# Layer A's attention: one sum product for two heads, and one store of a unit's two outputs into one tensor

## The chip, the core and the metric

The kernel runs on one core of a Trainium2 chip. The metric is the device time of one execution in microseconds (us), the median of several runs; lower is better.

## What is computed

A decoder trunk of two layers on one sequence of 2048 positions, model width 1024, all in float32. Layer A, where the change lies, is attention with a forget gate over 16 heads of width 64. Cut to what matters:

```python
# layer A
u = rmsnorm(h, norm_a_g)
q, k, v, f_logit, gate = jnp.split(u @ w_in_a, [1024, 2048, 3072, 3088], axis=-1)
q, k = rmsnorm(q.reshape(b, s, 16, 64), qnorm_g), rmsnorm(k.reshape(b, s, 16, 64), knorm_g)
c = jnp.cumsum(log_sigmoid(f_logit + b_forget), axis=1)
logits = q k^T / 8 + c[query] - c[key];  causal mask
o = softmax(logits) v
h = h + (o * silu(gate)) @ w_out_a
```

Layer B then computes a shared key/value projection, sliding-window attention and its own projection in the same style. Nothing of layer B's computation is changed.

## The kernel before

TensorE multiplies in fp32r. To keep float32 accuracy, an operand is split into a rounded high part and a rest, and a product is made of three: high by high, high by rest, rest by high. Tensors that do not fit on chip are spilled to DRAM and loaded again.

Layer A goes through four stages. **Projections** (`projections`, products at L759 and L722): q, k and v of all heads go to the DRAM tensors `qa`, `ka`, `va`, the running sums of the forget gate to `ca`, and the normed input to `ut`. **Attention** (`attention_a`): per head, four units of 512 queries (`CH`), per unit 2, 4, 6 or 8 steps of two key blocks of 128. A step makes the scores (L978, L979, with a mask added by a product with the identity matrix, L983 and L987), their exponentials on ScalarE (L984, L993), the high part (L996, ScalarE) and the rest (L997, GpSimd) of those, their running sum on VectorE (L1006), and three steps later the values products (L1021). Row maxima for heads further on are made beside it (L933, L941, L946) and are written into a row of the query operand by small transfers (`big<-m`, L560, four per unit). The **gate** (`gate()`, L1063) is a filler: its products are dealt out between the steps, and its weights come in through 62 loads of 512 KB into two `wr` buffers (`wr<-wg`, L1040).

At the end of a unit the sum of the exponentials is folded. VectorE's transposing reduction (L897) leaves in `part` 32-query pieces on 128 partitions; per head, `recips` makes one product with the constant `fold` (L906, 64 rows of 32), multiplies by `roots` (L911), takes the reciprocal (L912) and stores it to the DRAM tensor `rd` (L913). The last head does this in two parts. In the same place the unit's values leave PSUM by a ScalarE copy (L1029) into a tile of 128 rows: the upper 64 rows are the main part, the lower 64 the correction from the low part of v. They go out as two stores, to the DRAM tensors `om` (L1031) and `oc` (L1032), each [1024, 2048], 64 rows per head.

In the **output projection** (`out_a`, products at L1244) a step handles a chunk of 512 positions and a pair of heads, 32 steps in all. `gated_load` loads for a pair four tiles of 128 x 512: `m` from `om` (L1179), `c` from `oc` (L1180), the gate (L1181) and the reciprocals, spread over 64 rows each (L1184, two loads). `gated` adds m and c on GpSimd (L1198), multiplies by the reciprocals (L1199) and the gate (L1202), and splits the result (L1203, L1204) into the operand. Loads run five steps ahead and prepared operands two (`Pairs`); the first three pairs are loaded, and two of them prepared, within attention (L1198 to L1204 on GpSimd there). The residual x is loaded (L1229) and the result stored to `h1` (L1257) in the same stage.

All transfers are issued by SP in one queue, in order. The order on every engine is set when the program is built, by a scheduler that places instructions by its own estimates: when a product or a transfer goes away, its neighbours may change places.

Of the kernel before, what the change touches and what calls it, by code (L numbers as in the profile page):

```python
# [14 lines left out]
BF16 = mybir.dt.bfloat16  # L15
# [8 lines left out]
P = 128  # L24
S = 2048
# [126 lines left out]
class Trunk:  # L152
# [7 lines left out]
    def __init__(self, ctx, tc, a, out):  # L160
        self.ctx, self.tc, self.nc, self.a, self.out = ctx, tc, tc.nc, a, out
        dr = ctx.enter_context(tc.tile_pool(name="dram", bufs=1, space=DRAM))
        self.d = {
            name: dr.tile(shape, F32, name=name, tag=name)
            for name, shape in (
                ("qa", [H, P, S]),
                ("ka", [H, P, S]),
                ("va", [H, S, P]),
                ("ca", [2, H, S]),
                ("ut", [NCH, 2, NDT, P, CH]),  # L170
                ("wg", [NDT, P, 4, 2, 2, P]),
                ("gt", [D, S]),
                ("om", [D, S]),
                ("oc", [D, S]),
                ("rd", [H, S]),
                ("rr", [2, S]),
                ("h1", [S, D]),
                ("qb", [H, P, S]),
                ("kb", [NKV, P, S]),
                ("vb", [NKV, S, P]),  # L180
                ("gtb", [D, S]),
            )
        }
# [25 lines left out]
    def constants(self):  # L209
        nc, cp, a = self.nc, self.const, self.a  # L210

        def select(view, src, pattern, base, cm, fill):
            nc.gpsimd.affine_select(
                out=view, in_=src, pattern=pattern, compare_op=ALU.is_ge,
                fill=fill, base=base, channel_multiplier=cm,
            )

        def tile_(name, shape, dt=F32):
            return cp.tile(shape, dt, name=name, tag=name)

# [12 lines left out]
        self.identb = tile_("identb", [P, P], BF16)  # L233
        nc.vector.tensor_copy(self.identb, self.ident)

        self.mask_s = tile_("mask_s", [P, 2, P], BF16)
        nc.gpsimd.memset(self.mask_s, 0.0)
        for i in range(2):
            select(self.mask_s[:, i], self.mask_s[:, i], [[1, P]], 0, -1, NEG)

        self.band = tile_("band", [P, 2, P], BF16)
        nc.gpsimd.memset(self.band[:, 0], 0.0)
        select(self.band[:, 0, :], self.band[:, 0, :], [[-1, P]], 0, 1, NEG)
        nc.vector.tensor_tensor(self.band[:, 1], self.tri, self.ident, ALU.subtract)

        self.loads = []
        warm = tile_("warm", [P, 1])
        nc.scalar.activation(warm, self.ones[:, :1], AF.Sqrt)

        def vector(name, n, views):  # L250
            t = tile_(name, [P, n])
            for rows, src in views:
                self.loads.append((t[rows], src))
            return t

        def column(name, src, n):
            return vector(name, n, [(slice(0, P), src.rearrange("(t p) -> p t", p=P))])

        def pair_column(name, src):
            col = src.rearrange("(p o) -> p o", o=1)  # L260
            return vector(name, 1, [(slice(0, HD), col), (slice(HD, P), col)])

        def row(name, src, n):
# [585 lines left out]
    def attention_a(self, op):  # L849
# [12 lines left out]
            fill=NEG, base=0, channel_multiplier=1,  # L862
        )
        NSB = CH // 32
        part = self.sb("part", [P, 2, NCH, NSB], bufs=1)

        roots = self.sb("ro1", [NCH * NSB, 2, 32])
        heads, state = {}, {}
        units = [(h, ch) for h in range(H) for ch in range(NCH)]
        steps = [(u, p) for u, (h, ch) in enumerate(units) for p in range(2 * ch + 2)]  # L870
# [23 lines left out]
        def sums(u):  # L894

            h, ch = units[u]
            nc.vector.tensor_reduce(  # L897
                part[:, h % 2, ch, :], state[u][0].rearrange("p (b i) -> p b i", i=32),
                AX.X, ALU.add, apply_transpose=True,
            )  # L900

        def recips(h, c0=0, c1=NCH):

            nr = (c1 - c0) * NSB
            ps = self.ps("sc", [nr, 32])
            nc.tensor.matmul(  # L906
                ps, part[:, h % 2, c0:c1].rearrange("p c b -> p (c b)"), self.fold,
                start=True, stop=True,
            )
            rc = self.sb("sq", [nr, 32])  # L910
            nc.vector.tensor_tensor(rc, ps, roots[:nr, 1 if c0 else 0], ALU.mult)  # L911
            nc.vector.reciprocal(rc, rc)  # L912
            nc.sync.dma_start(  # L913
                out=d["rd"][h, c0 * CH : c1 * CH].rearrange("(b i) -> b i", i=32), in_=rc
            )

        def max_pieces(h, ch):
# [44 lines left out]
        def scores(n, u, p):  # L962
# [17 lines left out]

            if last:
                o = tiles[0].rearrange("p (b q) -> p b q", b=2)[:, :, :P]
                nc.tensor.matmul(o, self.identb, self.mask_s, start=False, stop=True)  # L983
                nc.scalar.activation(pf[:, :tw], tiles[0][:, :tw], AF.Exp, scale=HD**-0.5)  # L984
            else:
                for n_, ps in enumerate(tiles if diag else ()):
                    mm = nc.tensor.matmul(  # L987
                        ps[:, :P], self.identb, self.mask_s[:, 0], start=False, stop=True
                    )
# [21 lines left out]
        def values(item):  # L1011
# [14 lines left out]
            if last:  # L1026
                state.pop(u)
                ov = self.sb("sq", [P, CH])
                nc.scalar.copy(ov, pv)  # L1029
                rows, cols = slice(h * HD, (h + 1) * HD), slice(ch * CH, (ch + 1) * CH)  # L1030
                nc.sync.dma_start(out=d["om"][rows, cols], in_=ov[:HD, :])  # L1031
                nc.sync.dma_start(out=d["oc"][rows, cols], in_=ov[HD:, :])  # L1032

        def closes(item):
            u, p = item[:2]
# [58 lines left out]
        for c in range(2):  # L1094
            rows = roots[: (NCH - c) * NSB, c]
            nc.sync.dma_start(out=rows, in_=d["rr"][0, c * CH :].rearrange("(b i) -> b i", i=32))
            nc.vector.reciprocal(rows, rows)
        more_pieces(1)
        per = len(pieces)

# [32 lines left out]
        for n, (u, p) in enumerate(steps):  # L1133
# [12 lines left out]
            if p == 2 * ch + 1:  # L1146
                if h == H - 1 and ch in (0, NCH - 1):
                    due.append((n + SUM_LAG, (h, ch and 1, ch + 1)))
                elif ch == NCH - 1:
                    due.append((n + SUM_LAG, (h,)))  # L1150
            while due and due[0][0] <= n:
                recips(*due.pop(0)[1])
            feed((total - KEPT) * (n + 1) // len(steps), pause=True)
# [21 lines left out]
    def gated_load(self, ch, p, tiles):  # L1175
        nc, d = self.nc, self.d
        rows, cols = slice(p * P, (p + 1) * P), slice(ch * CH, (ch + 1) * CH)
        m, c, g, rb = tiles
        nc.sync.dma_start(out=m, in_=d["om"][rows, cols])  # L1179
        nc.sync.dma_start(out=c, in_=d["oc"][rows, cols])  # L1180
# [25 lines left out]
    def out_a(self, op, res, dst, ahead, fetch, norm):  # L1206
# [12 lines left out]
        for s in range(NCH * NDT):  # L1219
# [9 lines left out]
                nc.sync.dma_start(out=xr[:, p - 1], in_=res[t0 : t0 + P, :])  # L1229
            if s == NDT:  # L1230

                self.gk16 = self.sb("part", [P, ROT], bufs=1)
# [394 lines left out]
```

## Time and profile before

| | |
|---|---|
| Median of 3 runs | 2440.47 us (2437.79 to 2440.94) |
| Profiled execution | 2441.27 us, of which the span of the profile is 2439.5 us |
| Granted TensorE clock | 1.00 throughout |
| Attention (scores from 594 to 1434 us) | 595 to 1448 us |
| Output projection, first and last product | 1450.4 to 1626.3 us |
| SP: a store to `om`, a store to `oc`, a 128-row store to `gt` | medians 472, 588 and 326 ns of SP's time |

The span is the time from the first instruction to the last on the core. Busy time is the union of an engine's instructions; TensorE's ends are modelled, so its busy time says that it was fed, not that it ran at its peak. A row of a chain gives the start, the length and the engine, tile and line of a piece; the chain is followed back from the last instruction, at each step to what released it. A row of the waits reads: who waited, for whom, us in total, how often, the longest.

### The profile page before, as it was taken

The numbers are of one execution on the slowest core, as the hardware profiler recorded it, in microseconds if no ns is written. First come the engines' busy times: TensorE is split into PE (matmuls) and PEld (weight loads), VectorE is DVE, ScalarE is ACT, GpSimd is POOL, SyncE is SP. The second block draws the span as 40 slices with busy tenths as digits, with TensorE's granted clock in tenths as the row PEclk, the third lists the DMA queues.
The fourth block names the chain that finished last, engine by engine and source line by source line (L and its number), as shares of the span: only waits on it lengthen the run. The fifth ranks groups of instructions, "written<-read, shape, count | busy, mean of one in ns | idle before, by whom it ended". The sixth has DMA issues, their size and how long they took to land.

```text
span 2439.5 us, 36263 instructions
## 1 busy us (share of the span) xinstructions
PE 2407.4 (99%) x11952; PEld 2024.2 (83%) x11952; DVE 1729.3 (71%) x4098; ACT 1260.6 (52%) x2504; POOL 998.2 (41%) x643
## 2 busy tenths in 40 slices
PE   8999999999999999999999999999999999999999
PEld 6788899988888788888888778888888888788887
DVE  7656667735889888888988865556666523777776
ACT  5433324323878778777877761135322312555554
POOL 0000000011878777777878852200011000377775
PEclk9999999999999999999999999999999999999999
DMA  6656555677554655575466549965433425555552
GB/s 182 207 168 184 157 154 168 197 233 235 171 168 127 207 156 147 147 212 172 130 195 174 169 145 311 300 225 159 126 103 106 139 69 161 178 180 179 178 181 74
DMA packets 351517, 419.24 MB, mean 172 GB/s; under 512 B 64929, under 2 KB 248257, under 8 KB 345153
## 3 DMA queue, kind: packets, MB, share of 16 engines
q1 hardware_dynamic: 351328, 416.92, 57.2%
q8 instruction: 95, 1.56, 0.3%
q14 instruction: 94, 0.76, 0.1%
HBM read 265.29 MB, written 151.40 MB: 171 GB/s over the span
## 4 chain that ended last, share of the span: by engine, by line
PE 86%; DMA 5%; DVE 4%; ACT 2%; issue 1%; POOL 1%; SPq 1%; ACTq 0%; DVEq 0%; POOLq 0%
PE b L759 27%; PE pa L1021 10%; PE pb L1063 7%; PE b L1244 5%; PE pb L1457 5%; PE sc L978 5%; PE sc L979 5%; PE mx L933 5%; PE pb L722 3%; PE b L722 3%; PE pa L1387 2%; PE b L1308 2%; DMA wr<-wg 1%; PE pa L1244 1%; PE pb L1244 1%
## 5 line engine op out<-in xcount | busy, mean ns | idle before, releaser
L759 PE MATMUL b<-wh,big 128*128 128x512 f32 (+3 forms) x2560 | 774.1, 375 | 9.4 <-ACT wh L486 8.8
L997 POOL TENSOR_TENSOR big<-st,big 128x1024 fp32r<-128x1024 f32 (+1 forms) x320 | 655.4, 2067 | 242.5 <-ACT big L996 160.3
L759 PEld LDWEIGHTS b<-wh,big 128*128 128x128 f32 x2560 | 472.3, 189 | 82.2 <-ACT wh L486 10.9
L759 PE MATMUL b<-wl,big 128*128 128x512 f32 (+3 forms) x1280 | 474.9, 371 | 1.9 <-DVE wl L487 1.9
L1006 DVE TENSOR_TENSOR ac<-ac,st 128x512 f32<-128x512 f32 (+3 forms) x576 | 352.7, 612 | 51.7 <-ACT st L993 24.7
L993 ACT ACTIVATE st<-sc 128x512 f32<-128x512 f32 (+1 forms) x512 | 273.7, 583 | 117.8 <-PE sc L979 49.5
L1021 PE MATMUL pa<-big 128*128 128x512 f32 (+3 forms) x1280 | 319.9, 365 | 0.9 <-POOL big L997 0.9
L996 ACT CAST big<-st 128x1024 fp32r<-128x1024 f32 (+1 forms) x320 | 295.2, 923 | 8.5
L759 PEld LDWEIGHTS b<-wl,big 128*128 128x128 f32 x1280 | 241.9, 189 | 38.2 <-DVE wl L487 5.9
L1021 PEld LDWEIGHTS pa<-big 128*128 128x128 f32 x1280 | 229.2, 190 | 39.6 <-POOL big L997 2.7
L946 DVE TENSOR_REDUCE mt<-mx 128x1 f32<-128x384 f32 (+1 forms) x360 | 214.2, 598 | 29.5 <-PE mx L933 26.8
L495 ACT ACTIVATE sq<-b,r 128x512 f32<-128x512 f32 (+2 forms) x128 | 77.8, 608 | 301.1 <-PE b L759 298.2
L978 PE MATMUL sc<-big 128*128 128x512 f32 (+3 forms) x640 | 232.9, 368 | 0.1
L979 PE MATMUL sc<-big 67*128 67x512 f32 (+3 forms) x640 | 229.3, 367 | 0.0
L933 PE MATMUL mx<-big 66*128 66x512 f32 (+2 forms) x600 | 224.3, 379 | 0.2
L1063 PE MATMUL pb<-wh,wr 128*128 128x512 f32 x488 | 178.4, 398 | 4.2 <-DMA wr<-wg 4.0
L497 DVE TENSOR_REDUCE sm<-sq 128x8 f32<-128x512 f32 (+2 forms) x128 | 74.9, 585 | 138.4 <-ACT sq L495 138.2
L859 POOL MEMSET rot<- 128x512 bf16 x1 | 0.5, 524 | 421.2 <-PE pb L349 421.2
L1356 POOL TENSOR_TENSOR big<-big,tri 128x1024 fp32r<-128x1024 f32 x60 | 143.8, 2396 | 69.4 <-DVE big L1353 64.5
L941 DVE CUSTOM_DVE_ANT_0 mx<-mx,rot 128x384 f32<-128x384 f32 (+2 forms) x240 | 147.0, 617 | 20.7 <-PE mx L933 19.3
L978 PEld LDWEIGHTS sc<-big 128*128 128x128 f32 x640 | 121.7, 190 | 22.0 <-DVE st L542 0.5
L510 POOL TENSOR_TENSOR ro<-qn,rot 128x64 f32<-128x64 f32 (+1 forms) x48 | 15.6, 326 | 299.4 <-DVE qn L501 299.4
(281 smaller groups left out, 4226.5 us busy)
## 6 DMA issues: line engine op xcount, KB each, us to landing
wr<-wg SPq DMA_DIRECT2D x62, 512.0 KB
va<-st SPq DMA_DIRECT2D x32, 512.0 KB
ka<-st SPq DMA_DIRECT2D x64, 256.0 KB
ut<-big SPq DMA_DIRECT2D x16, 1024.0 KB
big<-ka SPq DMA_DIRECT2D x16, 1024.0 KB
big<-qa SPq DMA_DIRECT2D x16, 1024.0 KB
qb<-st SPq DMA_DIRECT2D x64, 256.0 KB
big<-qb SPq DMA_DIRECT2D x16, 1024.0 KB
```

The costliest lines, as they stand in the source:

```text
L759: nc.tensor.matmul(ps[:, :n], u[tb // 4][:, dt, us], W[k][dt], start=(dt == 0 and i == 0), stop=(dt == NDT - 1 and i == 2),)
L933: mm = nc.tensor.matmul(ps, qb[:66, i * P : (i + 1) * P], kb[:66, k0:k1], start=True, stop=True,)
L946: nc.vector.reduce_max(o, ps, axis=AX.X)
L978: nc.tensor.matmul(o, ka[:, ks], qa[:, qs], start=not (last and n_), stop=False)
L979: nc.tensor.matmul(o, kb[:, ks], qb[:, qs], start=False, stop=not diag)
L993: nc.scalar.activation(pf[:, off : off + w], ps[:, :w], AF.Exp, scale=HD**-0.5)
L996: nc.scalar.copy(ph[:, :tw], pf[:, :tw])
L997: nc.gpsimd.tensor_tensor(pl[:, :tw], pf[:, :tw], f_(ph[:, :tw]), ALU.subtract)
L1006: nc.vector.tensor_tensor(a_, a_, pf[:, off : off + w], ALU.add)
L1021: nc.tensor.matmul(pv[:, q0 : q0 + w], v[:, k, :], src[:, off : off + w], start=(p == 0 and n_ == 0 and i == 0), stop=(last and n_ == 1 an ...
L1063: nc.tensor.matmul(ps, w[:, dt // 2 % 2, wk, dt % 2, :], us[dt][uk], start=(dt == 0 and i == 0), stop=(dt == NDT - 1 and i == 2),)
L1244: nc.tensor.matmul(bank[tb][nh], op.y(s_)[:, k, tb * P : (tb + 1) * P], op.W[p_][:, j, nh * CH : (nh + 1) * CH], start=(p_ == 0 and i == 0 ...
```

## The change

Four edits, all in layer A's attention and what reads from it:

- `om` and `oc` become one tensor `oo` of [16, 128, 2048]: per head 64 main rows and then 64 correction rows. A unit's tile goes out as one store of 128 rows. The loads of a pair, still of 128 rows each, take 64 rows of one head and 64 of the next: on the DRAM side the pattern is now 2 heads by 64 rows by 512, with a step of 262,144 elements between the heads.
- `recips` can fold two heads in one product (128 rows) with one multiplication, one reciprocal and one store. It does so for heads 0 to 13 in pairs, when the second head of a pair is done; head 14 is folded alone and head 15 in two parts, as before. The sums of alternate pairs go to two `part` tiles, and `roots` is loaded a second time into partitions 64 to 127.
- The mask that is added to the last two blocks is kept once and read twice by a broadcast.
- `gk16` of layer B uses a buffer of `part`, of which there are now two.

```diff
-                ("om", [D, S]),
-                ("oc", [D, S]),
+                ("oo", [H, P, S]),
...
-        def recips(h, c0=0, c1=NCH):
-
-            nr = (c1 - c0) * NSB
+        def recips(h, c0=0, c1=NCH, n=1):
+
+            nr = n * (c1 - c0) * NSB
             ps = self.ps("sc", [nr, 32])
             nc.tensor.matmul(
-                ps, part[:, h % 2, c0:c1].rearrange("p c b -> p (c b)"), self.fold,
-                start=True, stop=True,
+                ps,
+                part[h // 2 % 2][:, h % 2 : h % 2 + n, c0:c1].rearrange("p n c b -> p (n c b)"),
+                self.fold, start=True, stop=True,
             )
...
             nc.sync.dma_start(
-                out=d["rd"][h, c0 * CH : c1 * CH].rearrange("(b i) -> b i", i=32), in_=rc
+                out=d["rd"][h : h + n, c0 * CH : c1 * CH].rearrange("n (b i) -> n b i", i=32),
+                in_=rc,
             )
...
-                rows, cols = slice(h * HD, (h + 1) * HD), slice(ch * CH, (ch + 1) * CH)
-                nc.sync.dma_start(out=d["om"][rows, cols], in_=ov[:HD, :])
-                nc.sync.dma_start(out=d["oc"][rows, cols], in_=ov[HD:, :])
+                nc.sync.dma_start(out=d["oo"][h, :, ch * CH : (ch + 1) * CH], in_=ov)
...
+        nc.sync.dma_start(out=roots[NCH * NSB :, 0], in_=d["rr"][0].rearrange("(b i) -> b i", i=32))
+        nc.vector.reciprocal(roots[NCH * NSB :, 0], roots[NCH * NSB :, 0])
...
-                elif ch == NCH - 1:
+                elif ch == NCH - 1 and h == H - 2:
                     due.append((n + SUM_LAG, (h,)))
+                elif ch == NCH - 1 and h % 2:
+                    due.append((n + SUM_LAG, (h - 1, 0, NCH, 2)))
...
-        nc.sync.dma_start(out=m, in_=d["om"][rows, cols])
-        nc.sync.dma_start(out=c, in_=d["oc"][rows, cols])
+        for k, t in enumerate((m, c)):
+            nc.sync.dma_start(
+                out=t, in_=d["oo"][2 * p : 2 * p + 2, k * HD : (k + 1) * HD, cols]
+            )
```

The order on SP in the output projection, before: the loads of two steps. `wh` and `wl` are the tiles, `om`, `oc`, `gt`, `rd` and `in_x` the DRAM tensors they come from.

```order
L1179 DMA wh<-om 128x512
L1180 DMA wl<-oc 128x512
L1181 DMA wh<-gt 128x512
L1184 DMA wl<-rd 64x512 x2
L128 DMA st<-in_w_out_a 128x1024
L1229 DMA big<-in_x 128x1024
L1179 DMA wh<-om 128x512
```

And at the same place now:

```order
L1183 DMA wh<-oo 128x1x512
L1183 DMA wl<-oo 128x1x512
L1186 DMA wh<-gt 128x512
L1189 DMA wl<-rd 64x512 x2
L128 DMA st<-in_w_out_a 128x1024
L1234 DMA big<-in_x 128x1024
L1183 DMA wh<-oo 128x1x512
```

The loads stand in the same order; the two of a pair now carry three dimensions, since the side in DRAM has three.

The order on SP near the end of attention, behind head 13's last units, before:

```order
L1031 DMA om<-sq 64x512
L1032 DMA oc<-sq 64x512
L913 DMA rd<-sq 64x32
L884 DMA big<-qa 128x2048
L560 DMA big<-m 1x128x1 x8
L1031 DMA om<-sq 64x512
L1077 DMA gt<-sq 128x512
L1032 DMA oc<-sq 64x512
L1040 DMA wr<-wg 128x1024 x2
```

And now:

```order
L1031 DMA oo<-sq 128x512
L882 DMA big<-qa 128x2048
L912 DMA rd<-sq 128x32
L1039 DMA wr<-wg 128x1024
L558 DMA big<-m 1x128x1 x8
L1031 DMA oo<-sq 128x512
L1076 DMA gt<-sq 128x512
L1039 DMA wr<-wg 128x1024
```

Each pair of stores has become one, and one of the two gate-weight loads (`wr<-wg`) now stands ahead of the eight small transfers of row maxima.

The order on TensorE behind head 0, before:

```order
L933 MATMUL mx<-big 128x512
L906 MATMUL sc<-fold,part 64x32
L1063 MATMUL pb<-wh,wr 128x512
L1063 MATMUL pb<-wl,wr 128x512
L933 MATMUL mx<-big 128x512
```

And now:

```order
L933 MATMUL mx<-big 128x512
L1062 MATMUL pb<-wh,wr 128x512
L1062 MATMUL pb<-wl,wr 128x512
L933 MATMUL mx<-big 128x512
L978 MATMUL sc<-big 128x256
```

The fold of an even head is gone and the rest moves up; a fold of 128x32 stands behind the next head.

More of the change, by code (lines that the diff above doesn't have):

```diff
@@ L234, in constants @@
         nc.vector.tensor_copy(self.identb, self.ident)
-        self.mask_s = tile_("mask_s", [P, 2, P], BF16)
+        self.mask_s = tile_("mask_s", [P, P], BF16)
         nc.gpsimd.memset(self.mask_s, 0.0)
-        for i in range(2):
-            select(self.mask_s[:, i], self.mask_s[:, i], [[1, P]], 0, -1, NEG)
+        select(self.mask_s, self.mask_s, [[1, P]], 0, -1, NEG)
         self.band = tile_("band", [P, 2, P], BF16)
@@ L864, in attention_a @@
         NSB = CH // 32
-        part = self.sb("part", [P, 2, NCH, NSB], bufs=1)
-        roots = self.sb("ro1", [NCH * NSB, 2, 32])
+        part = [self.sb("part", [P, 2, NCH, NSB], bufs=2) for _ in range(2)]
+        roots = self.sb("ro1", [P, 2, 32])
         heads, state = {}, {}
@@ L897, in sums @@
             nc.vector.tensor_reduce(
-                part[:, h % 2, ch, :], state[u][0].rearrange("p (b i) -> p b i", i=32),
+                part[h // 2 % 2][:, h % 2, ch, :], state[u][0].rearrange("p (b i) -> p b i", i=32),
                 AX.X, ALU.add, apply_transpose=True,
             )
-        def recips(h, c0=0, c1=NCH):
-            nr = (c1 - c0) * NSB
+        def recips(h, c0=0, c1=NCH, n=1):
+            nr = n * (c1 - c0) * NSB
             ps = self.ps("sc", [nr, 32])
             nc.tensor.matmul(
-                ps, part[:, h % 2, c0:c1].rearrange("p c b -> p (c b)"), self.fold,
-                start=True, stop=True,
+                ps,
+                part[h // 2 % 2][:, h % 2 : h % 2 + n, c0:c1].rearrange("p n c b -> p (n c b)"),
+                self.fold, start=True, stop=True,
             )
@@ L982, in scores @@
                 o = tiles[0].rearrange("p (b q) -> p b q", b=2)[:, :, :P]
-                nc.tensor.matmul(o, self.identb, self.mask_s, start=False, stop=True)
+                m = self.mask_s.unsqueeze(1).to_broadcast([P, 2, P])
+                nc.tensor.matmul(o, self.identb, m, start=False, stop=True)
                 nc.scalar.activation(pf[:, :tw], tiles[0][:, :tw], AF.Exp, scale=HD**-0.5)
@@ L987, in scores @@
                     mm = nc.tensor.matmul(
-                        ps[:, :P], self.identb, self.mask_s[:, 0], start=False, stop=True
+                        ps[:, :P], self.identb, self.mask_s, start=False, stop=True
                     )
@@ L1230, in out_a @@
             if s == NDT:
-                self.gk16 = self.sb("part", [P, ROT], bufs=1)
+                self.gk16 = self.sb("part", [P, ROT], bufs=2)
                 gk = self.a["knorm_b_g"].rearrange("(o d) -> o d", o=1)[:, :ROT]
```

## The prediction

> **What bounds the kernel now.** I read the page first, then the stretches by stage, then the waits and the single lines of the stage that the change touches. From the page, busy time and the DMA totals:
>
> ```profile
> span 2439.5 us, 36263 instructions
> PE 2407.4 (99%) x11952; PEld 2024.2 (83%) x11952; DVE 1729.3 (71%) x4098; ACT 1260.6 (52%) x2504; POOL 998.2 (41%) x643
> DMA packets 351517, 419.24 MB, mean 172 GB/s; under 512 B 64929, under 2 KB 248257, under 8 KB 345153
> ```
>
> From the table of stretches, attention (595 to 1448 us), the output projection of layer A, and that stage's last 10 us. The columns are length, then busy time with count of PE, PEld, DVE, ACT and POOL, then granted clock, busy share of the 16 DMA engines, GB/s:
>
> ```profile
> 595.00:1448.00 853.00, 847.57 (x4142) 699.76 (x4141) 742.78 (x1626) 673.28 (x1063) 666.58 (x329) 1.00 0.58 166
> 1450.00:1610.00 160.00, 159.14 (x702) 131.47 (x701) 89.99 (x121) 26.89 (x41) 37.96 (x29) 1.00 1.00 305
> 1600.00:1610.00 10.00, 10.00 (x45) 8.27 (x45) 6.88 (x10) 4.49 (x8) 1.29 (x1) 1.00 1.05 380
> ```
>
> TensorE sets the time in both stages. In attention the DMA engines have room (0.58). In the output projection they have none: share 1.00, while TensorE is busy 159.14 of 160 us. So this stage stands at the edge of a second bound, and the change rewrites two of its loads. The lines of that stage's loads, adds and use, each from the view of one source line (minimum/median/maximum ns, then first and last start in us):
>
> ```profile
> L1179 SPq DMA_DIRECT2D wh<-om x29: 325/374/1149, 1374.4 to 1594.2; - x29
> L1180 SPq DMA_DIRECT2D wl<-oc x29: 319/357/1143, 1448.0 to 1594.8; - x29
> L1198 POOL TENSOR_TENSOR wh<-wh,wl x29: 1271/1289/1732, 1451.6 to 1602.0; 128x512 f32<-128x512 f32 x29
> L1204 DVE TENSOR_TENSOR big<-wh,big x29: 683/692/1617, 1459.5 to 1606.3; 128x512 fp32r<-128x512 f32 x29
> ```
>
> The last add starts at 1602.0, so its loads have landed by then; the last operand is split by 1606.3 + 0.7 = 1607.0. The chain that ended last shows when TensorE comes to it, and what one step takes (4.08 + 0.68 + 0.68 = 5.44 us):
>
> ```profile
> 1614.94 4.08 PE b L1244 x18
> 1619.02 0.68 PE pa L1244 x3
> 1619.70 0.68 PE pb L1244 x3
> 1620.38 4.08 PE b L1244 x18
> ```
>
> The operand waits 13.4 us for TensorE (1620.4 - 1607.0). That is all the cover these loads have at the end of the stage. GpSimd, which makes the add, already waits for the loads, so they land only just ahead:
>
> ```profile
> POOL wh L1198 <- DMA wl<-oc: 117.1, 26, 13.1
> ```
>
> **The change part by part.** *The folds.* Seven of 17 products L906 go, with 14 small VectorE operations and 7 stores. A fold on TensorE, in the chain and in its line:
>
> ```profile
> 655.21 0.28 PE mx L933
> 655.49 0.23 PE sc L906 x2
> 655.72 0.66 PE pb L1063 x2
> L906 PE MATMUL sc<-fold,part x34: 193/223/243, 655.4 to 1444.7; 128*64 128x32 f32 x30, 128*16 128x32 f32 x2, 128*48 128x32 f32 x2
> ```
>
> It takes 0.23 us of the chain, and at most 2 x 0.22 = 0.45 us by its two records. Seven give 1.6 to 3.1 us on the path. Seven of the ten that are left load 128 weight columns in place of 64, which takes back a little; I take 3, as the record after a fold is late too. The VectorE work lies beside TensorE (742.78 of 853 us busy) and counts nothing.
>
> *The stores.* 64 stores fewer leave SP's queue, and rd stores no longer stand ahead of some gate-weight loads. What TensorE can win from that is all it now loses to those loads:
>
> ```profile
> PE pb L1063 <- DMA wr<-wg: 4.0, 5, 1.6
> ```
>
> Bounds 0 and -4.0 us. In attention the loads of pairs 0 to 2 meet the new form below and may hold up a weight load by up to 5.5 us each; bounds 0 and +11. I put these two against each other at zero. The mask that is read twice in place of being kept twice, the third reciprocal of `roots`, and one memset and select less on POOL lie under TensorE's first stretch and get zero: the products keep their count and shape.
>
> *The loads.* Before, `om` and `oc` gave each load 128 rows at one stride on both sides. Now the rows of two heads are 64 and 64 with a gap, so on the DRAM side the outermost dimension counts 2. Is such a transfer still spread over 16 engines? The trace of before has one kind whose outermost dimension counts 2, the load of the two forget rows (2x2048), 16 of them. From the DMA issues (count, KB each):
>
> ```profile
> wr<-wg SPq DMA_DIRECT2D x62, 512.0 KB
> ...
> big<-m SPq DMA_DIRECT2D x256, 0.5 KB
> ...
> big<-ca SPq DMA_DIRECT2D x16, 16.0 KB
> ...
> part<-in_knorm_b_g SPq DMA_DIRECT2D x1, 8.0 KB
> ```
>
> The view's rows sum to 1,505 transfers (first and last are shown). Those made of pieces under 512 B (from `big<-m`, 256 x 128 pieces of 4 B, to `part`, 128 rows of 64 B) give 38,400 of 4 B, 1,536 of 64 B and 1,136 of 128 B, 41,072 packets. If every transfer also ended with one small packet on each of 16 engines, that adds 24,080, in all 65,152. The page has 64,929: 223 fewer. If the 16 `ca` loads run on 2 engines each, 16 x 14 = 224 are missing. So a transfer whose outermost dimension counts 2 uses 2 engines, and the rest, with 16, 48, 64 or 128 there, use 16. For 2 on one side and 128 on the other there is no row; the bounds are 2 engines and 16. I take 2, as the side that counts 2 cannot be dealt out further at that dimension.
>
> The Trainium skill, page "DMA: Bandwidth & Descriptors", section "Why a DMA increments its semaphore by 16 and not by 1", states it as a rule: the engine count is the largest number up to 16 that divides the slowest dimension of both sides. By that rule 2 and 128 give 2, and the sum is the one below; without it, the first rival's. The trace agrees for `ca` (223 packets short).
>
> Now the price, on the two engines that must carry every such load. The loads and stores of the stage, from the same view:
>
> ```profile
> wl<-rd SPq DMA_DIRECT2D x64, 128.0 KB
> big<-in_x SPq DMA_DIRECT2D x16, 512.0 KB
> h<-big SPq DMA_DIRECT2D x16, 512.0 KB
> wh<-om SPq DMA_DIRECT2D x29, 256.0 KB
> wl<-oc SPq DMA_DIRECT2D x29, 256.0 KB
> wh<-gt SPq DMA_DIRECT2D x29, 256.0 KB
> ```
>
> Per step and engine: the two attention outputs, 512 KB on 2 engines, 262,144 B. The rest, gt 256 + rd 256 + x 256 + h1 256 = 1,024 KB on 16 engines, 65,536 B. Together 327,680 B. An engine moves 380/16 = 23.75 GB/s in the best stretch above, 305/16 = 19.1 over the stage. I take the best, since 14 engines now idle and contend less: 13.8 us per step against TensorE's 5.44. From 1448.0 on, 29 loads of `oc` and 28 of `om` are still to come (one was issued at 1374.4), 28.5 pairs: 393 us, so the last lands at 1841 instead of 1602, 239 us later. Of this the 13.4 us of cover is used up: +226. After waiting TensorE starts slow, as the chain shows at the program's start against later:
>
> ```profile
> 12.84 5.18 PE b L759 x14
> 117.50 5.46 PE b L759 x24
> ```
>
> 0.37 us a product against 0.23: +3 us for the last step's 24; the earlier ones (24 x 0.37 = 8.9 us) still fit into 13.8.
>
> The same page gives about 27 GiB/s for an engine (section "Specifications"). An estimate by it is 11.3 us per step, a last landing near 1770 and a time near 2595; the trace's best 10 us show 23.75 GB/s, and I stay with that.
>
> The sum against the profiled execution, 2441.3 us (1.8 of it outside the span): 2441.3 + 226 + 3 - 3 = 2667. It lies 0.8 above the median 2440.5, so 2666. Bounds: with the 262,144 B alone, 11.0 us a step, 314 us, the end at 1762: +147, time 2585. At 19.1 GB/s, 17.2 us a step, 490 us, end at 1938: +323, time 2764; with the 11 us in attention, 2775.
>
> **The rivals.** *All 16 engines carry the load* (the DRAM side is dealt out by rows, not by its outer two). Then the projection keeps its 5.44 us steps, and only the folds and the queue are left: -3 us and 0 to -4 more, 2433 to 2438, about 2436. For it: each piece is still a full 2 KB row, the bytes are the same, and no row shows 2 against 128. Against it: the 223 missing packets. The point from which it decides is at four engines: there the two outputs take 131,072 B per engine and step, with the rest 196,608, 8.3 us, still above 5.44; at eight engines 131,072, 5.5 us, the two meet. *The change's own aim, larger than I think*: with 16 engines, the weight waits go whole and the folds cost their upper price, -7, 2433; it is the lower half of the first rival. *Two engines, but GpSimd's earlier adds block attention*: GpSimd makes the add and the fp32r rest (L997) in one queue, so an add that waits for a load on two engines holds back the values products. Three pairs are loaded there, each 2 x 5.5 us: if none is covered, +33, about 2699. Against it: the loads stand well ahead of the adds in SP's order, and GpSimd is busy only 666.58 of 853 us; it lies within the range.
>
> **How the numbers follow.** A measurement of this kernel can tell about 0.2% from no change, 4.9 us (the three runs lie 3.2 apart). Two engines: 0.87, of which 0.05 for the blocked adds. All 16: 0.13, half of it beyond -4.9 us (0.06), half within (0.07). The range 2585 to 2775 takes in the price bounds of the likely case and leaves out the other, 0.13, and a little more at the upper end. So faster 0.06, same 0.07, slower 0.87.
>
> **What would show it.** Right: TensorE idle in the output projection with the adds L1203 of the new listing waiting for `oo`, the stage stretched from about 175 to about 400 us, a low DMA share (about 0.3) with about 120 GB/s (305 x 160 / 400), and under-512-B packets fewer by 14 for each `oo` load. Attention, to about 1450, shorter by 0 to 5 us. Wrong: a stage of 175 us with share near 1.00 (the first rival), or a stretched stage whose waits end on something else than `oo`.

## The result, and the profile after

| | before | after |
|---|---|---|
| Median | 2440.22 us (5 runs, 2437.79 to 2440.94) | 2678.43 us (5 runs, 2676.79 to 2683.12) |
| Ratio | | 1.0986, 95% interval 1.0974 to 1.0997 |
| Span of the profile | 2439.5 us | 2676.3 us |
| Scores of attention, first start to last end | 594.3 to 1434.4 us | 596.6 to 1451.8 us |
| Output projection, first to last product | 1450.4 to 1626.7 us | 1467.8 to 1864.9 us |
| Rest of the program | 812.7 us | 811.4 us |

The changed kernel is 238 us slower, against the 226 of the forecast. From the page of after, the span, busy time and the DMA totals:

```profile
span 2676.3 us, 36148 instructions
PE 2457.6 (92%) x11938; PEld 2056.2 (77%) x11938; DVE 1724.2 (64%) x4085; ACT 1260.7 (47%) x2504; POOL 997.9 (37%) x642
PEclk9999999999999999999999776777999999999999
DMA packets 349563, 419.24 MB, mean 157 GB/s; under 512 B 62976, under 2 KB 246304, under 8 KB 343200
```

TensorE's share falls from 99 to 92%, and the DMA engines move the same 419.24 MB more slowly on average. The row of the clock by fortieths of the span shows where: a dip of six slices, behind the middle. The table of stretches, with the columns as in the prediction (length, busy time and count of PE, PEld, DVE, ACT, POOL, clock, DMA share, GB/s), for attention and the output projection:

```profile
595.00:1448.00 853.00, 832.56 (x4059) 690.80 (x4058) 729.28 (x1600) 664.50 (x1050) 658.99 (x325) 0.99 0.54 164
1450.00:1850.00 400.00, 232.83 (x825) 179.72 (x823) 94.09 (x129) 31.81 (x48) 41.48 (x32) 0.77 0.39 127
```

The projection takes 397 us for what took 176. TensorE is busy 233 of 400 us, no other engine more than that, and the DMA engines show a share of 0.39 at 127 GB/s where they had 1.00 at 305: a stage that waits for transfers while the DMA engines look idle, because the share is a mean over 16. The longest waits of the stage, then the line of GpSimd's adds (minimum/median/maximum ns, first and last start) and what it sat idle for:

```profile
ACT big L1208 <- DVE wh L1207: 355.6, 27, 23.1
POOL wh L1203 <- DMA wl<-oo: 297.8, 24, 16.7
DVE wh L1204 <- POOL wh L1203: 221.0, 23, 12.0
PE b L1249 <- DVE big L1260: 76.4, 4, 30.7
...
PE b L1249 <- ACT big L1208: 60.7, 11, 11.5
```

```profile
L1203 POOL TENSOR_TENSOR wh<-wh,wl x29: 1261/1262/1295, 1471.5 to 1851.5; 128x512 f32<-128x512 f32 x29
...
  DMA wl<-oo: 297.8, 24
```

Read the waits from the far end: TensorE for the operand's high part, ScalarE for VectorE, VectorE for GpSimd's add, the add for the load of `oo`, 24 times, 298 us in all (117.1 us before, when the loads landed just ahead). TensorE's largest single item, 76.4 us in four waits, is for L1260, VectorE's addition of the residual, which frees a bank of PSUM; the first L1260 starts at 1570.2, right behind the operand of a later step (L1209) in VectorE's order, so it stood behind the same late loads. The last add starts at 1851.5 where it started at 1602.0. The chain that ended last shows its cause:

```profile
1829.49 21.89 DMA wl<-oo
1851.53 1.27 POOL wh L1203
1852.83 0.70 DVE wh L1204
1853.55 0.70 DVE wh L1207
```

The last load of corrections is under way for 21.9 us. By the price of the forecast, 131,072 B at 24 GB/s on each of two engines, it would take 5.5 us alone; the rest it stands behind others on the same engines. The records of single packets, counted by their start and length, show how many engines these are: from 1480 to 1840 us there are never fewer than two packets in flight, and exactly two for 57% of the time. Loads that count 16 are late too: in the chain from 1450 to 1866 us, 26.6% lie in the loads of `rd`, 19.0% in those of the corrections and 10.3% in those of the gate, since a part of each goes to the two full engines. SP, which issues the loads, shows the same from the other side:

```profile
L1183 SPq DMA_DIRECT2D wh<-oo x32: 512/536/872, 1293.4 to 1828.9; - x32
L1183 SPq DMA_DIRECT2D wl<-oo x29: 567/4909/6399, 1463.0 to 1829.5; - x29
L1186 SPq DMA_DIRECT2D wh<-gt x29: 375/5024/7342, 1464.8 to 1836.0; - x29
```

The issue of the second load of a pair takes SP a median of 4.9 us; before it took 0.36 (L1180). The gate's load behind it takes another 5.0 us, so SP is held for some 10 us of a step. Two packets are in flight all the while, so no gap on the two full engines shows.

### The profile page after: what moved, and what is told of

The parts are those of the page before. It is cut to its first block, busy times and chain, and to the rows that moved or that the text cites. A ratio compares the mean times of both kernels' runs of the same rounds, so it can differ in the third digit from the quotient of the medians.

```text
span 2676.3 us, 36148 instructions
## 1 busy us (share of the span) xinstructions
PE 2457.6 (92%) x11938; PEld 2056.2 (77%) x11938; DVE 1724.2 (64%) x4085; ACT 1260.7 (47%) x2504; POOL 997.9 (37%) x642
## 2 busy tenths in 40 slices
DMA packets 349563, 419.24 MB, mean 157 GB/s; under 512 B 62976, under 2 KB 246304, under 8 KB 343200
## 4 chain that ended last, share of the span: by engine, by line
PE 70%; DMA 14%; DVE 6%; SPq 3%; ACT 3%; issue 2%; POOL 2%; DVEq 0%; ACTq 0%; POOLq 0%
PE b L757 25%; PE pa L1022 9%; PE pb L1062 6%; PE sc L978 5%; PE sc L979 5%; PE mx L933 4%; DMA wl<-rd 4%; PE pb L1462 4%; PE pb L720 3%; DMA wl<-oo 3%; PE b L720 2%; DMA wh<-gt 2%; SPq L1186 1%; PE pa L1392 1%; PE b L1313 1%
## 5 line engine op out<-in xcount | busy, mean ns | idle before, releaser
L757 PE MATMUL b<-wh,big 128*128 128x512 f32 (+3 forms) x2560 | 774.0, 375 | 13.5 <-ACT wh L484 11.3
L998 POOL TENSOR_TENSOR big<-st,big 128x1024 fp32r<-128x1024 f32 (+1 forms) x320 | 655.9, 2069 | 240.4 <-ACT big L997 157.6
L1249 PE MATMUL b<-big 128*128 128x512 f32 x576 | 182.0, 480 | 171.8 <-DVE big L1260 76.4
L1022 PE MATMUL pa<-big 128*128 128x512 f32 (+3 forms) x1280 | 317.3, 366 | 15.5 <-POOL big L998 15.5
L1249 PEld LDWEIGHTS b<-big 128*128 128x128 f32 x576 | 136.1, 241 | 215.2 <-ACT big L1208 65.4
L1022 PEld LDWEIGHTS pa<-big 128*128 128x128 f32 x1280 | 230.1, 190 | 55.0 <-POOL big L998 18.3
L1204 DVE TENSOR_TENSOR wh<-wh,wl 128x512 f32<-128x512 f32 x29 | 20.1, 692 | 280.7 <-POOL wh L1203 221.0
L1208 ACT CAST big<-wh 128x512 fp32r<-128x512 f32 x29 | 17.9, 618 | 355.7 <-DVE wh L1207 355.6
L1203 POOL TENSOR_TENSOR wh<-wh,wl 128x512 f32<-128x512 f32 x29 | 36.8, 1268 | 360.1 <-DMA wl<-oo 297.8
```

The lines of the kernel that those rows point to most:

```text
L757: nc.tensor.matmul(ps[:, :n], u[tb // 4][:, dt, us], W[k][dt], start=(dt == 0 and i == 0), stop=(dt == NDT - 1 and i == 2),)
L998: nc.gpsimd.tensor_tensor(pl[:, :tw], pf[:, :tw], f_(ph[:, :tw]), ALU.subtract)
L1022: nc.tensor.matmul(pv[:, q0 : q0 + w], v[:, k, :], src[:, off : off + w], start=(p == 0 and n_ == 0 and i == 0), stop=(last and n_ == 1 an ...
L1249: nc.tensor.matmul(bank[tb][nh], op.y(s_)[:, k, tb * P : (tb + 1) * P], op.W[p_][:, j, nh * CH : (nh + 1) * CH], start=(p_ == 0 and i == 0 ...
```

## The experiments

Theory: the load with 2 rows of 64 on the DRAM side runs on 2 of 16 engines, and only that costs time. Rivals: (A) its pieces lie too far apart in DRAM; (B) the single store or the folds cost it; and, for attention, (C) the rival of the forecast, GpSimd's early adds.

### The load cut into halves, each one head

The changed kernel with

```diff
-            nc.sync.dma_start(
-                out=t, in_=d["oo"][2 * p : 2 * p + 2, k * HD : (k + 1) * HD, cols]
-            )
+            for s in range(2):
+                nc.sync.dma_start(
+                    out=t[s * HD : (s + 1) * HD],
+                    in_=d["oo"][2 * p + s, k * HD : (k + 1) * HD, cols],
+                )
```

> The changed kernel, but each of the two loads of a pair is cut at the head: 64 rows from one head and 64 from the next, so the outermost dimension counts 64 on both sides. One store, one tensor, paired folds and the addresses read in DRAM stay. Theory (the loads run on two DMA engines because their outermost dimension counts 2): the output projection goes back to 5.44 us a step and about 176 us, the DMA share there to about 1.00; what is left is the gain of the folds and the queue, 2433 to 2440 us, I expect 2436. Rival A (two pieces of DRAM 1 MB apart are slow to read, or one tensor is): the addresses are the same, so it stays near 2678. Rival B (the single store or the folds cost the time): also near 2678.

Measured: 2449.74 us (ratio 1.0043, 1.0029 to 1.0056), the projection 185.0 us. The page has 64,896 packets under 512 B, 62,976 + 64 x 14 + 64 x 16, as it must be if 128 loads on 16 engines stand where 64 on 2 stood. The same rows from the same places, by twice as many loads, give back 229 of 238 us: A and B fall for the loss as a whole. The time lies above the 2433 to 2440 expected: some 12 us remain against the kernel before; the runs below come back to them.

### The folds alone

The kernel before with the paired folds (`recips`, `part`, `roots` and `due` as in the change), and the change's mask that is kept once; stores and loads of the outputs as before.

> The changed kernel with om and oc, their two stores and their two loads as before; the paired folds, the mask kept once and the second part tile stay. It measures the fold's half of the change alone. Theory: seven folds fewer at 0.23 to 0.45 us each, and weight loads that no longer stand behind their stores (0 to 4.0 us): 2433 to 2439 us, I expect 2437, ratio 0.997 to 1.000. Rival B (the folds cost something): 2441 or more.

Measured: 2438.11 us (0.9997, 0.9988 to 1.0006): no difference. The 1.6 to 3.1 us do not show, though the interval, -2.9 to +1.5 us, allows for most of them. In the one profile of each kernel, the weight-load waits of the gate are 8.2 us here, where they were 4.0:

```profile
PE pb L1065 <- DMA wr<-wg: 8.2, 6, 2.9
```

### The load's form alone, on two and on four engines

The kernel before, folds and tensors as before, but with one unused row behind every 64 (or 32) rows of `om` and `oc`, so that a pair's load counts 2 by 64 (or 4 by 32) in DRAM. No two neighbouring rows are more than one unused row apart. In the kernel with four, a unit's outputs go out as four stores of 32 rows. For two:

```diff
-                ("om", [D, S]),
-                ("oc", [D, S]),
+                ("om", [D // 64, 65, S]),
+                ("oc", [D // 64, 65, S]),
...
-        nc.sync.dma_start(out=m, in_=d["om"][rows, cols])
-        nc.sync.dma_start(out=c, in_=d["oc"][rows, cols])
+        for name, t in (("om", m), ("oc", c)):
+            nc.sync.dma_start(out=t, in_=d[name][2 * p : 2 * (p + 1), :64, cols])
```

> The kernel before, with one unused row put behind every 64 rows of om and oc. The stores stay two of 64 rows, the folds stay 17; the load of a pair must now step over the unused row, so that its outermost dimension counts 2, and the two pieces lie 8 KB apart instead of 1 MB. Theory: two engines as in the changed kernel, 13.6 to 13.8 us a step, packets under 512 B 14 fewer for each of the 64 loads (64,929 - 896 = 64,033), time 2670 to 2690 us. Rival A (far pieces): near 2441. Rival B (store or folds): near 2441.

> The kernel before, with one unused row behind every 32 rows of om and oc. A load's outermost dimension counts 4; a unit's outputs go out as four stores of 32 rows. Theory: four engines carry the two outputs, per engine and step 131,072 + 65,536 B, at 23.75 GB/s 8.3 us; 28.5 steps take 236 us instead of the 154 of before, less 13.4 us of cover: 2500 to 2525 us, I expect 2511; packets under 512 B fall by 12 for each of the 64 loads and rise by 16 for each of 128 more stores: 64,929 - 768 + 2,048 = 66,209. A rival by which the three-dimensional form as such is slow, and not the count of engines, gives 2678 again.

Measured: 2675.61 us with two, as expected, and 2541.4 us with four, above the 2500 to 2525 expected; one run each. The pages' DMA totals of two, then of four:

```profile
DMA packets 350620, 419.24 MB, mean 157 GB/s; under 512 B 64032, under 2 KB 247360, under 8 KB 344256
```

```profile
DMA packets 352797, 419.26 MB, mean 165 GB/s; under 512 B 66208, under 2 KB 249536, under 8 KB 346432
```

64,032 and 66,208 small packets stand against 64,033 and 66,209 expected, if a load that counts 2 ends with one small packet on each of 2 engines and one that counts 4 on each of 4. And one unused row in the layout of before makes the whole loss of the change. The packet records agree: from 1480 to 1710 us of the four-engine kernel there are never fewer than four packets in flight. That kernel came out 30 us above the 2511 expected: attention ends 12 us later than before, and the loads go slower than priced. The lines of the loads of `oc` and of the adds (first and last start at the end), of two:

```profile
L1184 SPq DMA_DIRECT2D wl<-oc x29: 560/4835/6094, 1463.4 to 1827.1; - x29
```

```profile
L1202 POOL TENSOR_TENSOR wh<-wh,wl x29: 1261/1262/1297, 1471.7 to 1848.6; 128x512 f32<-128x512 f32 x29
```

and of four:

```profile
L1184 SPq DMA_DIRECT2D wl<-oc x29: 536/550/3067, 1460.0 to 1700.6; - x29
```

```profile
L1202 POOL TENSOR_TENSOR wh<-wh,wl x29: 1259/1284/1296, 1465.9 to 1715.4; 128x512 f32<-128x512 f32 x29
```

From the first load to the last add, over 28.5 steps: two engines 385.2 us, 13.5 a step; four 255.4 us, 9.0 a step, where 8.3 were priced.

### The load on eight engines

One unused row behind every 16 rows, loads of 8 by 16; first with eight stores of 16 rows per unit, then with two stores of 4 by 16.

> The kernel before, with one unused row behind every 16 rows of om and oc; a pair's load then counts 8 by 16 rows, and each unit's outputs go out as eight stores of 16 rows. Theory (a transfer runs on as many engines as its outer count, here 8): the two outputs put 65,536 B on each of 8 engines per step and the rest 65,536 B, 131,072 B at 23.75 GB/s = 5.5 us, level with TensorE's 5.44: time 2440 to 2455, a stage of 176 to 190 us, packets under 512 B 64,929 - 8 x 64 + 16 x 384 = 70,561. Rival (it is the gap between the rows, or the number of dimensions, that slows a transfer, whatever the count): as with four and two outer rows, 2540 or more.

> As the kernel with one unused row behind every 16 rows of om and oc, but each unit's two outputs go out as two stores again, of 4 by 16 rows, in place of eight stores of 16 rows. The loads count 8. Theory (a transfer runs on as many engines as its outer count): the loads put 131,072 B with all the rest on the busiest engines per step, 5.5 us, so the projection takes 176 to 192 us; the stores run on 4 engines, 128 KB in 1.4 us, short beside the 13 us of a unit, and attention loses less than 15 us: time 2440 to 2465, packets under 512 B 64,929 - 64 x 8 - 128 x 12 = 62,881. Rival (the 250 us of the kernel with eight stores come from the loads): time above 2600, the projection above 300 us.

Measured: 2687.08 us with eight stores (1.1017, 1.0998 to 1.1035), 2507.14 us with two (1.0288, 1.0272 to 1.0303). Both miss their expectation. Of the first there is no profile that can be compared with the others stage by stage, so where its 248 us go is left open (its packets under 512 B, 70,560 against 70,561 expected, fit the count); since the same loads with two stores cost 69 us, most of it goes with the eight stores. Of the second, the loads of `oc` and the adds:

```profile
L1183 SPq DMA_DIRECT2D wl<-oc x29: 594/600/1012, 1485.5 to 1670.5; - x29
```

```profile
L1201 POOL TENSOR_TENSOR wh<-wh,wl x29: 1259/1288/1920, 1490.5 to 1681.2; 128x512 f32<-128x512 f32 x29
```

195.7 us over 28.5 steps are 6.9 a step, where 5.5 were priced, and the projection takes 210.6 us; the other 33 us are lost in attention. Its stores on 4 engines and its early loads on 8 are both new there, and no run tells them apart. The count holds, with 62,881 small packets as expected, and from 1490 to 1670 us fewer than eight packets are in flight for 0.5% of the time. What was wrong is the price: the rate of one engine is not the same when two or eight of them are loaded.

| loads on | bytes per step on a loaded engine | us a step | GB/s of one engine |
|---|---|---|---|
| 2 (after) | 327,680 | 13.6 | 24.0 |
| 2 (gap of a row) | 327,680 | 13.5 | 24.2 |
| 4 | 196,608 | 9.0 | 21.9 |
| 8 | 131,072 | 6.9 | 19.1 |

The rate is the priced bytes by the time of a step, and since as many packets as loaded engines were in flight nearly all the time, idle engines are unlikely to explain its fall. The stage moves a few per cent more than was priced, so the rates are a little low. 19.1 is also 305/16, the rate of before with all 16 at work. The best stretch, 23.75, was the right row for two engines and the wrong one for eight.

### The slow form moved from the load to the store

The changed kernel with `oo` laid out as pair, kind, 128 rows: loads whole, and the one store of a unit counts 2 by 64.

```diff
-                nc.sync.dma_start(out=d["oo"][h, :, ch * CH : (ch + 1) * CH], in_=ov)
+                s = h % 2 * HD
+                nc.sync.dma_start(
+                    out=d["oo"][h // 2, :, s : s + HD, ch * CH : (ch + 1) * CH], in_=ov
+                )
```

> The changed kernel, with oo laid out as pair, kind, 128 rows: the loads are whole again (128 rows at one stride), and the one store of a unit now counts 2 by 64 rows. Theory (a slow transfer costs only where somebody waits for it and its two engines have no room): the 64 stores run on two engines, 256 KB at 23.75 GB/s in two halves = 5.5 us each, one per 13 us of attention where the DMA engines are busy 0.58: the projection returns to 176 us, attention gains or loses less than 15 us, time 2438 to 2455; packets under 512 B fall by 64 x 14 = 896 against the same kernel with 16 engines. Rival (two engines make a transfer slow for everyone behind it in SP's order): each store holds up the weight and key loads behind it, 64 x up to 5.5 = up to 350 us, time well above 2500.

Measured: 2536.70 us (1.0401, 1.0385 to 1.0416), a clear miss, on the rival's side of 2500. The packet count, 62,977 under 512 B where 62,976 were expected, says that now the stores run on two engines. The projection comes back to 182.9 us, but attention takes 931.7 us in place of 840.1. A piece of its chain of waits, in the stretch from 830 to 846 us:

```profile
830.70 11.21 DMA oo<-sq
...
842.04 0.69 DVE sq L1076
...
843.99 0.56 DVE sq L1078
844.55 0.04 issue
844.59 1.65 PE pb L1065 x3
```

The store takes 11.2 us and holds its `sq` tile. There are two of these (`SLOTS`), shared by the units' copies, the gate and the reciprocals: the gate's next tile waits for the store, and TensorE's gate product for that. The waits of the kernel add the weight loads, which ran 4.0 us late before:

```profile
PE pb L1065 <- DMA wr<-wg: 24.7, 8, 5.9
```

In attention as a whole, the stores of `oo` are 8.5% of the chain (79 us), and the weight loads 7.2% (67 us) where they were 3.6% (30 us). So the theory, that a slow transfer costs only where somebody waits for it, left out who waits for a store: the next writer of its tile. How much of the 92 us is this and how much the delay of the weight loads behind the stores, which was the rival, is not told apart; no run has more `sq` tiles.

### Only the early pairs cut

The changed kernel with the three pairs that are loaded within attention cut by heads (`if ch == 0 and p < 3`), the other 29 as the change has them.

> The changed kernel, with only the three pairs that are loaded within attention cut into loads of 64 rows per head; the other 29 steps load as the change does. Theory (attention's 17 us come from GpSimd's adds that wait for the slow loads of pairs 0 to 2, and hold back the values products): scores end at 1434 to 1437 in place of 1451.8, the projection still takes 390 to 400 us, time 2660 to 2666. Rival (the 17 us come from the folds, the store or the longer queue): scores end at 1448 to 1453, time 2676 to 2682.

Measured: 2661.41 us, one run, within the 2660 to 2666 expected; scores end at 1432.4 (1451.8 in the changed kernel) and the projection takes 399.7 us. The 17 us of attention are rival C. In the changed kernel's waits within attention and, from the line L1203 there, what its adds sat idle for:

```profile
PE pa L1022 <- POOL big L998: 15.2, 4, 10.6
```

```profile
  DMA wh<-oo: 11.3, 1
  DMA qn<-oo: 6.4, 1
```

Two of the three early adds wait 11.3 and 6.4 us for their loads; the rests of the exponentials (L998) stand behind them on GpSimd, and TensorE's values products (L1022) behind those.

### The kernel before with its loads cut

For the 12 us that the cut loads left: `om` and `oc` as before, each load in two of 64 rows.

> The kernel before, with each load of om and oc cut into two of 64 rows, nothing else: 64 more transfers, packets under 512 B 64,929 + 64 x 16 = 65,953. Theory (the 9 us that the projection lost with cut loads come from the number of transfers in a stage whose DMA engines are full): time 2446 to 2451, the projection 183 to 187 us. Rival (they come from the single store or from the layout of oo): time 2438 to 2441, the projection 176 us.

Measured: 2455.93 us (1.0071, 1.0056 to 1.0086), above the 2446 to 2451 expected, the projection 187.8 us: what the projection lost with cut loads lies with them, not with the store or with `oo`. Of the 13.5 us by which the span grew, 11.5 lie there and 3.6 behind it, where the cause is open. Stretches of 100 us in that stage, of the kernel before, of this one, and of the changed kernel with cut loads:

```profile
1500.00:1600.00 100.00, 100.00 (x443) 82.81 (x442) 48.85 (x70) 11.75 (x20) 23.20 (x18) 1.00 1.01 297
```

```profile
1500.00:1600.00 100.00, 92.92 (x394) 75.89 (x393) 50.99 (x66) 10.55 (x17) 22.76 (x17) 0.97 0.94 259
```

```profile
1500.00:1600.00 100.00, 94.22 (x400) 77.03 (x399) 51.66 (x67) 10.56 (x18) 22.89 (x17) 0.97 0.96 266
```

The DMA share falls by 5 to 7% and the rate by 10 to 13%. So the engines are both less filled and slower at a packet: one of 2,048 B takes 117 ns in the mean in the kernel before, and 126 and 125 ns in the two others. Why is open; SP's issue of a cut load takes 0.59 us, where a 128-row load took 0.36.

### Main and correction rows in turns

A layout in which both transfers can have one stride: interleave the columns of v (main part i in column 2i, its correction in 2i+1). A unit's tile then holds main and correction rows in turns; the store is 128 rows in order, and a pair's load is 128 rows at a stride of two.

```diff
+        order = "p h (d k) -> p h d k" if turns else "p h (k d) -> p h d k"
+        hi, lo = (st.rearrange(order, k=2)[:, :, :, k] for k in range(2))
...
-                out=t, in_=d["oo"][2 * p : 2 * p + 2, k * HD : (k + 1) * HD, cols]
+                out=t, in_=d["oo"].rearrange("h (i k) s -> (h i) k s", k=2)[rows, k, cols]
```

The first of three kernels has layer B's v in turns too, though its readers take halves, so layer B's result there is not the reference's. The second has layer A's alone; the third is the second with the folds and the mask as before.

> The changed kernel with the columns of v interleaved (column 2i is v's main part i, column 2i+1 its correction i), so that main and correction rows of a head alternate in oo: the one store of a unit is still 128 rows in order, and a pair's load is 128 rows at one stride of two rows. Theory (only the count of 2 in the load cost time): all transfers on 16 engines, packets under 512 B 62,976 + 64 x 14 = 63,872, the projection 175 to 178 us, attention to 1433 to 1437, time 2433 to 2441, no different from the kernel before or a few us under it. Rival (the pieces of a load that are two rows apart, or writes of v at a stride of two elements, cost time themselves): time 2445 or more, with the projection above 180 us or the scores starting after 598.

> As alternate_rows, but only layer A's v has its main and correction columns in turns; layer B's keeps the halves that its readers take. Theory (only the count of 2 in the load cost time; without it the change is worth its folds and its one store, 0 to 5 us): the projection 175 to 178 us, attention to 1432 to 1437, time 2433 to 2439, ratio 0.997 to 1.001. Rival (writes of v at a stride of two elements, or rows two apart, cost time): time above 2443, scores starting after 597 or a projection above 180 us.

> The kernel before with one store per unit into oo and main and correction rows in turns, the folds one per head as before. It splits the last run's difference: if the folds are worth the 1.6 to 3.1 us of the forecast, this kernel is that much slower than the one with the folds paired, 2436 to 2441; if the folds are worth nothing here (as they were beside two stores), the two agree within 1.5 us.

Measured: 2436.66 us (0.9991, 0.9982 to 1.0000), 2436.89 us (0.9992, 0.9983 to 1.0001) and 2439.12 us (1.0005, 0.9995 to 1.0015). The DMA totals of the second:

```profile
DMA packets 350459, 419.24 MB, mean 172 GB/s; under 512 B 63872, under 2 KB 247200, under 8 KB 344096
```

The kernel has the same transfers as the changed one, save for the stride in the loads, and 63,872 - 62,976 = 896 = 64 x 14 small packets more: the 64 loads of `oo` run on 16 engines here and ran on 2 there. The projection takes 176.2 us. With the loads repaired the change is level with the kernel before; the 2.2 us between the second and the third kernel are of the size of the folds' price, but their intervals overlap, so the folds' worth stays undecided.

## Why the prediction was right

*The engine count.* Taken as 2 between bounds of 2 and 16, from 223 missing packets. Shown: 896 packets fewer than the same kernel at one stride, the two packets in flight, and the one-row gap, which makes the same loss. The rule of the Trainium skill that it set beside this (page "DMA: Bandwidth & Descriptors", section "Why a DMA increments its semaphore by 16 and not by 1") agrees with the counts for 2, 4 and 8 against 128. The 27 GiB/s that the Trainium skill gives for an engine (same page, section "Specifications") were not reached: two engines moved 24.0 to 24.2 GB/s each, 13.6 us a step against the 11.3 estimated by it.

*The price.* 13.8 us a step were forecast and 13.6 measured, 388 us from the first load to the last add against 393. The mechanism is the one forecast: two full engines set the step, also for the loads that count 16. That the price came within 1% was partly luck. Its 23.75 was read off 10 us with all 16 engines at work, and the same rate was too high by a quarter for eight engines. The reason given, that idle engines contend less, fits the fall of the rate in the table. That SP would be held for 10 us of each step was not in the forecast, and cost nothing.

*The start.* The forecast began the loads at 1448.0; they began at 1463.0, since attention ran 15 us longer (855.2 to 840.1 us). Here a step failed, though the time stayed within the range: weight waits and early loads were put "against each other at zero". The early loads cost 15 to 17 us (the run with only these cut ends its scores 19 us earlier), above the 11 given as their bound, because the price was put on weight loads and the cost came through GpSimd's queue. That is the third rival, held at 0.05 with +33 if none of the three pairs was covered; two were uncovered in part. The evidence against it (loads well ahead of the adds in SP's order, GpSimd not full) spoke of averages, and one add that waits is enough.

*The cover and the slow start.* Forecast: 13.4 us used up and 3 lost on TensorE's slow start, together the stage ending 10.4 us closer to its last add. Measured: 24.7 us from last add to last product before (1626.7 - 1602.0), 13.4 after (1864.9 - 1851.5), 11.3 closer. In time order, TensorE's last products of the stage:

```profile
1854.95 6.79 PE L1249 MATMUL b<-big 128*128 128x512 f32 x18 [8.44 <-ACT big L1208]
```

18 products in 6.79 us, 0.377 each, where 0.37 was read off the program's start.

*The folds and the stores.* Forecast -3 for the folds; alone they gave nothing that could be measured. With one store beside them the kernel was 1.8 us below the kernel before, an interval that just takes in 1. The term of 3 us was not confirmed: it lies just outside the interval of the folds alone, and in a sum some eighty times larger its error could not be seen.

The sum closes: the span grew by 236.8 us, of which 2.3 before attention, 15.1 in it, 220.8 in the projection (397.1 - 176.3) and -1.3 behind. Forecast from 2667: +226. The terms that missed are the start (+15) and the folds (+3), less the shorter steps (-5), the cover (-1) and the rest of the program (-1): the 11 us between 226 and 236.8.

*What would show it* came as written: adds waiting for `oo`, a stage near 400 us, 127 GB/s for the "about 120" forecast. The share was 0.39 rather than 0.3, and attention grew where it was to shrink.

## What to carry to other kernels

Before two transfers are merged or a tensor is laid out anew, look at the outermost count of both sides of every transfer that touches it: a load of 128 rows that counts 2 by 64 on one side is a two-engine transfer, and the page shows it as fewer small packets and a DMA share that looks low while everything waits. A stage whose DMA share is near 1.00 pays for any such loss at once. A stage with room can pay too: through the queue in which a waiting add stands (17 us here), or through the tile that a slow store holds and the loads behind it (92 us together). Price an engine by a stretch in which as many engines are loaded as will be.

## What the runs showed of the hardware

- The rate of one DMA engine, as worked out in the table, fell from 24 GB/s with two loaded to 19.1 with eight.
- SP is held while it issues to two loaded engines: the second load of a pair took a median of 4.91 us to issue (4.84 with the one-row gap), 0.55 with four engines and 0.60 with eight. The gate's load behind it, on 16 engines, took 5.02.
- Granted clock fell while TensorE waited: 0.77 over the projection of the changed kernel, 0.88 and 0.93 with four and eight engines, 1.00 when fed. The stretches of four and eight:

```profile
1466.00:1715.00 249.00, 194.09 (x740) 150.57 (x738) 81.17 (x114) 23.56 (x36) 35.80 (x28) 0.88 0.60 191
```

```profile
1485.00:1680.00 195.00, 172.55 (x716) 139.86 (x715) 83.72 (x116) 23.66 (x36) 37.34 (x28) 0.93 0.80 239
```
